# Gate and z projections as one 512-column product, a branch hint and neighbouring value products, in a four-layer kernel

## The chip, the cores and the metric

The kernel runs on one core of a Trainium2 chip. The metric is the device time of one execution in microseconds. TensorE (PE, with its weight loads as PEld), VectorE (DVE), ScalarE (ACT), GpSimd (POOL) and SyncE (SP, whose queue issues the DMAs) run side by side and wait for each other by semaphores.

## The reference

256 tokens of width 1024 pass through four layers, all in float32. The first two are hybrid layers, the last two a mixing attention with a hierarchical mixture of experts. Cut to what matters:

```python
def hybrid_layer(x, ...):                         # twice
    h = rms_norm(x, norm_g)
    (qa, ka, va, za, ba, aa, ub, zb, qc, kc, vc, zc, iq, ik, iw, gates) = split_columns(h @ w_in)
    ya = deltanet_branch(qa, ka, va, za, ba, aa, ...)      # ... * silu(za)
    yb = pooling_branch(ub, zb, ...)                       # ... * silu(zb)
    yc = sparse_attention_branch(qc, kc, vc, zc, ...)      # ... * silu(zc)
    projected = einsum('btnc,ncd->btnd', stack([ya, yb, yc]), w_branch)
    gate = sigmoid(gates.reshape(b, t, 3, 1024) + gate_b)
    return x + sum(gate * projected, axis=2) @ w_out

def second_block(x, ...):                         # two layers
    h = _mixing(x, ...)       # 4 heads each: stick-breaking, forgetting, MLA, dilated (3 branches)
    x = _layernorm(alpha * x + h, ln1_g, ln1_b)
    m = _hier_moe(x, ...)     # 16 experts, two for each token
    x = _layernorm(alpha * x + m, ln2_g, ln2_b)
```

The gates have 3 x 1024 columns and za, zb, zc 512 each.

## The kernel before

**Products.** A float32 product that must be exact is done in three: both operands are split into a rounded part (`hi`, by a cast on ACT, L383) and the rest (`lo`, a subtraction on DVE or POOL, L384), and `mm3` adds hi times hi, hi times lo and lo times hi. Weights come through SP's queue in tiles `w` of 512 KB and are split on the way.

**Projections.** `proj_t` keeps the weights stationary (128 rows of the output at a time) and lets the 256 tokens move; it makes one output tile of 128x256 in 8 steps of three products. Two such tiles share a PSUM bank `pd` of 512 columns, of which there are three, and `use` reads both when the second is done. `gates` (tanh of each of 8 tiles, L951) and the calls for za, zb and zc (`silu2`, L662 and L663) go through it; the gates are multiplied into the branch products at L962 and L965. `proj_n` keeps the tokens stationary and lets 512 weight columns move.

**Attention.** `heads` handles two heads at a time and both query blocks (128 and 256 keys): softmax of a head, transposes of its weights `p` on TensorE (L368) and copies of them into `pt` on ACT (L1093, L1095). `weigh` then multiplies by the values (mv, vv, and x for the dilated heads), with two heads in the two halves of the array's columns. Forgetting, MLA and dilated heads go through it, two pairs each in a layer.

**Experts.** 16 experts are worked in pairs from slots of 64 tokens. `stream` issues the expert weights ahead of their use, into tiles that earlier stages free, in the order of `SLOTS_W` and `SLOTS_1` and with the buffers of `TWO`. At the ninth expert (`e == 8`) `overflow` has a conditional for tokens beyond the slots:

```python
n = nc.values_load(mi[0:1, 0:1], skip_runtime_bounds_check_because="compared only")
...
with tc.If(n > SLOTS):
```

Its body is skipped in these runs, so that TensorE branches over it (L1740). The router's product is made with 120 columns, six copies of 20.

**Order.** A scheduler sets the order of the instructions on each engine ahead of time, by the dependences and its own estimates; the source's order is only one input.

Of the kernel before, what the change touches and what calls it, by code (L numbers as in the profile page):

```python
# [49 lines left out]
TWO = dict(w4=18, w4b=5, w2=4, w2a=6, w2b=6, w1=2, w1a=6, w1b=4, wo=4, hi=3, lo=3)  # L50
# [3 lines left out]
SLOTS_W = [("w4", 8)] * 18 + [("w4b", 8)] * 5 + [("w2", 4)] * 4 + [("w2b", 4)] * 6 + [("ring", 8)] * RING  # L54
# [181 lines left out]
class K:  # L236
# [92 lines left out]

    def s(self, name, *shape, bufs=2, dt=F32):  # L330
        return self.sm.tile([128] + list(shape), dt, name=name, bufs=bufs)
# [74 lines left out]
    def proj_t(self, blk, l, name, act, use, per=1):  # L406

        kk = len(act[0])
        i, ps = 0, None
        for hi, lo in self.group(blk, l, name):  # L410
            v = [a.rearrange("p (k n) -> p k n", k=kk) for a in (hi, lo)]
            for j in range(per):
                if i % 2 == 0:
                    ps = self.dbank()
                o = ps[:, (i % 2) * T:(i % 2) * T + T]
                cs = slice(j * 128, j * 128 + 128)
                for k in range(kk):
                    self.mm3(o, (v[0][:, k, cs], v[1][:, k, cs]), (act[0][k], act[1][k]), k == 0, k == kk - 1)
                if i % 2:
                    use(i - 1, ps[:, 0:T])  # L420
                    use(i, o)
                i += 1
# [85 lines left out]
    def transposed(self, src, name, scale=None, bias=None, keep=True, banks=(None,)):  # L508
# [3 lines left out]
        hi, lo = self.big(name + "h", 8, F32R), self.big(name + "l", 8, F32R)  # L512
# [21 lines left out]
        return full, (hi, lo)  # L534
# [48 lines left out]
    def layer1(self, l):  # L583
# [338 lines left out]
        pt("zb", lambda i, ps: silu2(zb[:, i], ps, w1("sz")))  # L922
# [25 lines left out]
        def gates(n):  # L948
# [6 lines left out]
            pt("g%d" % n, use)  # L955
# [19 lines left out]
        pt("zc", lambda i, ps: silu2(zc[:, i], ps, w1("sz")))  # L975
# [40 lines left out]
        pt("za", lambda i, ps: silu2(za[:, i], ps, w1("sz")))  # L1016
# [23 lines left out]
    def layer2(self, l, xT, xs):  # L1040
# [37 lines left out]
        def heads(scale, logits, nbr=1, pair=None):  # L1078


            pts = [(w4("pt2")[:, :768], w2("pt1")[:, :384]) if nbr == 3 else (w2("pt")[:, :384],) for _ in range(2)]
            at = lambda j, br: pts[j][br // 2][:, (br % 2) * 384:(br % 2) * 384 + 384]

            def rest(j, qb, parts):
                S = 128 * (qb + 1)
                p = (w4 if nbr == 3 else w1)("p")[:, :nbr * S]
                self.softmax(parts, scale, p)
                for br in range(nbr):
                    pst = bank()
                    for i in range(qb + 1):  # L1090
                        self.tr(pst[:, tok(i)], p[:, br * S + i * 128:br * S + i * 128 + 128])
                    if qb:
                        A.copy(at(j, br)[:, 128:384], pst[:, 0:256])  # L1093
                    else:
                        A.copy(at(j, br)[:, 0:128], pst[:, 0:128])  # L1095

            if pair:
                for qb in range(2):
                    for j, parts in enumerate(pair(qb)):
                        rest(j, qb, parts)  # L1100
            else:
                for j in range(2):
                    for qb in range(2):
                        rest(j, qb, logits(j, qb))
            return [[at(j, br) for br in range(nbr)] for j in range(2)]
# [258 lines left out]
        for tb in range(2):  # L1364
            for k in range(8):
                self.mm(pl[:, tb * 120:tb * 120 + 120], zT[k // 4][tb][:, k % 4],
                        gw[:, k, None, :].to_broadcast([128, 6, 20]), k + tb == 0, k == 7)
# [25 lines left out]
    def moe(self, l, zh, lg):  # L1393
# [252 lines left out]
        for e in range(0, NE, 2):  # L1646
# [23 lines left out]
            if e % 4 == 2 and e + 2 < NE:  # L1670
                next_Ds, next_Db, _ = one_hot(e + 2)
                nxt = self.chunks("xg")
                for at, k in ((3, 0), (3, 2), (6, 4), (6, 6)):
                    todo_b.setdefault(at, []).append(lambda k=k: gather((k, k + 1), next_Ds, nxt))
            into_slots(e + 1, todo_b)
# [44 lines left out]
    def overflow(self, l, cnt, G2, zs, pv, sums):  # L1720
# [19 lines left out]
        with tc.If(n > SLOTS):  # L1740
# [100 lines left out]
```

## Time and profile before

| | |
|---|---|
| median of 3 runs | 1511.82 us (1511.78 to 1512.58) |
| profiled execution | 1510.49 us |
| its span | 1508.1 us |
| hybrid layers | about 0 to 645 us |
| attention stages | about 645 to 845 and 1065 to 1270 us |
| expert layers | about 845 to 1065 and 1270 to 1495 us |
| TensorE, VectorE, ScalarE busy | 97%, 53%, 44% of the span |
| mean granted clock of TensorE | 0.993 |

The span is what the trace covers; the execution's own time has some 2.4 us more around it. Names of rows are the program's tiles: `pd<-hTh,hi` is a product into bank pd of the token part hTh and the weight part hi (hTl and lo are the rests), and L349 is the line of the helper that records each product. The printed end of a product is modelled and overlaps with the next one, so its pace is read from the starts.

### The profile page before, as it was taken

To read this page: it belongs to the slowest core of one execution; us is meant where nothing else is said; L and a number is where in the kernel's file an instruction comes from. 1 tells how busy PE (TensorE), PEld (TensorE's weight loads), DVE (VectorE), ACT (ScalarE), POOL (GpSimd) and SP (SyncE) were. 2 spreads that over 40 slices of the span, in tenths; PEclk is the share of its full clock that TensorE was granted. 3 is DMA by queue.
4 is the path that set the end of the run, shared out by engine and by line. 5 is a ranking of instruction groups with operands and counts; after the bars stand their busy time and mean duration, and the time that the engine had idled before them with its cause. 6 is when DMAs were issued, how large, how long until landed. Compare 5 with 4: busy or idle time off the path is not lost. (4 is left out here: it accounts for less than half of the span.)

```text
span 1508.1 us, 25410 instructions
## 1 busy us (share of the span) xinstructions
PE 1461.3 (97%) x9770; PEld 1074.5 (71%) x9770; DVE 802.5 (53%) x1865; ACT 667.2 (44%) x1359; POOL 87.2 (6%) x94
## 2 busy tenths in 40 slices
PE   8999999999999999999999999899899999998996
PEld 7878999989788999987777644343677877443442
DVE  5878656669768556766754511111656655211113
ACT  6635545557555455456564311111465563111111
POOL 3300000111100000020000100000100001000000
PEclk9999999999999999999999999999999999999998
DMA  7522664555225655544578889999334778989994
GB/s 270 170 59 66 206 184 140 179 156 178 88 62 166 192 160 163 175 129 152 165 269 292 296 344 396 406 408 404 118 118 145 247 264 311 361 346 404 404 405 167
DMA packets 108144, 345.49 MB, mean 229 GB/s; under 512 B 12144, under 2 KB 16880, under 8 KB 108016
## 3 DMA queue, kind: packets, MB, share of 16 engines
q1 hardware_dynamic: 108016, 343.79, 65.5%
q8 instruction: 80, 1.31, 0.3%
q14 instruction: 48, 0.39, 0.1%
HBM read 342.69 MB, written 1.05 MB: 228 GB/s over the span
## 5 line engine op out<-in xcount | busy, mean ns | idle before, releaser
L384 DVE TENSOR_TENSOR lo<-w,hi 128x1024 fp32r<-128x1024 f32 (+3 forms) x243 | 298.6, 1229 | 164.8 <-ACT hi L383 160.2
L383 ACT CAST hi<-w 128x1024 fp32r<-128x1024 f32 (+2 forms) x258 | 268.0, 1039 | 230.7 <-PE pd L349 182.6
L349 PE MATMUL p<-w,xg 128*64 128x512 f32 (+1 forms) x1028 | 234.9, 595 | 8.1 <-issue 4.1
L349 PE MATMUL pd<-hTh,hi 128*128 128x256 f32 x768 | 218.7, 285 | 0.0
L349 PE MATMUL pd<-hTl,hi 128*128 128x256 f32 x768 | 218.2, 284 | 0.0
L349 PE MATMUL pd<-hTh,lo 128*128 128x256 f32 x768 | 218.2, 284 | 0.0
L349 PEld LDWEIGHTS p<-w,xg 128*64 128x64 f32 x1028 | 72.8, 137 | 130.3 <-issue 110.4
L349 PEld LDWEIGHTS pd<-hTl,hi 128*128 128x128 f32 x768 | 147.2, 192 | 0.2
L349 PEld LDWEIGHTS pd<-hTh,hi 128*128 128x128 f32 x768 | 147.2, 192 | 0.2
L349 PEld LDWEIGHTS pd<-hTh,lo 128*128 128x128 f32 x768 | 147.2, 192 | 0.1
L349 PE MATMUL p<-w,hTe 128*64 128x512 f32 x512 | 117.8, 594 | 0.0
L1626 DVE SCALAR_TENSOR_TENSOR yl<-p,gslot,yh 128x512 fp32r<-128x512 f32 x32 | 24.0, 751 | 143.4 <-ACT yh L1625 116.3
L349 PEld LDWEIGHTS p<-w,hTe 128*64 128x64 f32 x512 | 37.0, 137 | 72.2 <-issue 64.6
L349 PE MATMUL pd<-hi,xTh 128*128 128x512 f32 (+2 forms) x224 | 87.2, 389 | 0.1
L349 PE MATMUL pd<-hi,xTl 128*128 128x512 f32 (+2 forms) x224 | 86.5, 388 | 0.0
L349 PE MATMUL pd<-lo,xTh 128*128 128x512 f32 (+2 forms) x224 | 85.4, 381 | 0.0
L1580 ACT COPY a<-p 128x512 f32<-128x512 f32 x32 | 18.8, 586 | 147.1 <-PE p L349 146.6
L1590 DVE SCALAR_TENSOR_TENSOR t<-t,p 128x256 f32<-128x256 f32 x32 | 13.4, 419 | 122.2 <-ACT t L1589 113.8
L1625 ACT ACTIVATE yh<-p,gslot 128x512 fp32r<-128x512 f32 x32 | 22.0, 688 | 101.0 <-PE p L349 87.7
L349 PE MATMUL pd<-hi,hTl 128*128 128x512 f32 (+1 forms) x160 | 63.4, 398 | 0.0
L349 PE MATMUL pd<-lo,hTh 128*128 128x512 f32 (+1 forms) x160 | 61.9, 387 | 0.5 <-POOL lo L384 0.5
L349 PE MATMUL pd<-hi,hTh 128*128 128x512 f32 (+1 forms) x160 | 62.1, 388 | 0.0
(540 smaller groups left out, 2780.9 us busy)
## 6 DMA issues: line engine op xcount, KB each, us to landing
w<-in_we SPq DMA_DIRECT2D x320, 512.0 KB, 8.9
w<-in_p SPq DMA_DIRECT2D x244, 512.0 KB, 3.7
w<-in_we SPq DMA_DIRECT2D x110, 256.0 KB, 6.4
w<-in_p SPq DMA_DIRECT2D x8, 420.0 KB, 3.5
w<-in_we SPq DMA_DIRECT2D x20, 128.0 KB, 5.3
x<-in_we SPq DMA_DIRECT2D x4, 512.0 KB, 4.0
w<-in_p SPq DMA_DIRECT2D x4, 498.0 KB, 4.9
x<-in_x SPq DMA_DIRECT2D x4, 256.0 KB, 4.1
```

Source lines behind the costliest of these rows:

```text
L349: self.last = self.nc.tensor.matmul(out, lhsT, rhs, start=start, stop=stop, skip_group_check=True)
L383: r = self.nc.scalar.copy(hi, a)
L384: (eng or self.nc.vector).tensor_tensor(lo, a, hi.bitcast(F32), op=OP.subtract)
L1580: A_.copy(a, ps)
L1590: V.scalar_tensor_tensor(t, t, 1.0, ps[:, :, 0:64], op0=OP.add, op1=OP.mult)
L1625: A_.activation(yh, ps, AF.Copy, scale=gs)
L1626: V.scalar_tensor_tensor(yl, ps, gs, yh.bitcast(F32), op0=OP.mult, op1=OP.subtract)
```

## The change

Four edits:

1. For the gates and za, zb, zc the two token parts lie side by side in one tile (`parts`), and the high weights multiply both in one product of 512 columns; the low weights times the high tokens are added onto the second half. The two halves are added behind: ACT copies the first out of the bank, DVE adds the second. Each output tile then has a bank of its own, and tanh and silu read the sum from SBUF.
2. TensorE gets a hint that the branch over the overflow's body is likely taken.
3. `heads` takes both heads of a query block together: their transposes go to one bank, one ACT copy takes them out, and all transposes of a block stand together. Buffers `w4` fall from 18 to 15 and `w4b` rise from 5 to 8.
4. The router's product has 20 columns, not 120.

```diff
@@ -47,11 +47,11 @@
 
 ONE = dict(w4=14, w4s=2, w2=4, w2n=11, w2s=1, w1=14, w1n=13, w1s=3, hi=3, lo=3, j=1)
 ONE_P = dict(pd=3, p=2, pn=3)
-TWO = dict(w4=18, w4b=5, w2=4, w2a=6, w2b=6, w1=2, w1a=6, w1b=4, wo=4, hi=3, lo=3)
+TWO = dict(w4=15, w4b=8, w2=4, w2a=6, w2b=6, w1=2, w1a=6, w1b=4, wo=4, hi=3, lo=3)
 MIX_P = dict(pd=2, p=1, pa=2, pb=3)
 MOE_P = dict(p=4, pacc=4)
 
-SLOTS_W = [("w4", 8)] * 18 + [("w4b", 8)] * 5 + [("w2", 4)] * 4 + [("w2b", 4)] * 6 + [("ring", 8)] * RING
+SLOTS_W = [("w4", 8)] * 15 + [("w4b", 8)] * 8 + [("w2", 4)] * 4 + [("w2b", 4)] * 6 + [("ring", 8)] * RING
 
 SLOTS_1 = [("wo", 8)] * 2 + [("hi", 8), ("lo", 8)] + [("w1", 2)] * 2 + [("w1a", 2)] * 6 + [("w1b", 2)] * 2 + [("w2a", 4)] * 5 + [("x", 8)] * 2
 
@@ -327,6 +327,13 @@
         ts = [self.w4(name, 4, T, dt=dt) for _ in range((n + 3) // 4)]
         return [ts[i // 4][:, i % 4] for i in range(n)]
 
+    def parts(self, name, n):
+
+
+        ts = [self.w4(name, 2, 2 * T, dt=F32R) for _ in range((n + 1) // 2)]
+        both = [ts[i // 2][:, i % 2] for i in range(n)]
+        return [a[:, :T] for a in both], [a[:, T:] for a in both], both
+
     def s(self, name, *shape, bufs=2, dt=F32):
         return self.sm.tile([128] + list(shape), dt, name=name, bufs=bufs)
 
@@ -403,9 +410,22 @@
         for j, n in enumerate(ns):
             yield self.piece(self.I["p%d" % blk][l, i0 + j, :, :n], n, name)
 
-    def proj_t(self, blk, l, name, act, use, per=1):
+    def proj_t(self, blk, l, name, act, use, per=1, into=None):
+
 
         kk = len(act[0])
+        if into:
+            for i, (hi, lo) in enumerate(self.group(blk, l, name)):
+                v = [a.rearrange("p (k n) -> p k n", k=kk) for a in (hi, lo)]
+                ps = self.dbank()
+                for k in range(kk):
+                    self.mm(ps, v[0][:, k], act[2][k], k == 0, False)
+                    self.mm(ps[:, T:], v[1][:, k], act[0][k], False, k == kk - 1)
+                o = into(i)
+                self.nc.scalar.copy(o, ps[:, :T])
+                self.nc.vector.tensor_tensor(o, o, ps[:, T:], op=OP.add)
+                use(i, o)
+            return
         i, ps = 0, None
         for hi, lo in self.group(blk, l, name):
             v = [a.rearrange("p (k n) -> p k n", k=kk) for a in (hi, lo)]
@@ -509,7 +529,7 @@
 
         V, A, G = self.nc.vector, self.nc.scalar, self.nc.gpsimd
         full = self.big(name, 8) if keep else [None] * 8
-        hi, lo = self.big(name + "h", 8, F32R), self.big(name + "l", 8, F32R)
+        parts = hi, lo, _ = self.parts(name + "p", 8)
         col = lambda a, c: a[:, c:c + 1]
         for c in range(8):
             ps = self.bank(banks[c % len(banks)])[:, :T]
@@ -531,7 +551,7 @@
         if keep and bias is None:
             for c in range(8):
                 G.tensor_tensor(full[c], hi[c].bitcast(F32), lo[c].bitcast(F32), op=OP.add)
-        return full, (hi, lo)
+        return full, parts
 
     def rope(self, dst, src, cos, sin, half):
 
@@ -919,7 +939,7 @@
         V.tensor_scalar(hps, pv["pool_scale"], 0.5, None, op0=OP.mult)
         ob = (w4("obh", 4, T, dt=F32R), w4("obl", 4, T, dt=F32R))
         zb = w4("zb", 4, T)
-        pt("zb", lambda i, ps: silu2(zb[:, i], ps, w1("sz")))
+        pt("zb", lambda i, o: silu2(o, o, w1("sz")), into=lambda i: zb[:, i])
         pls = []
         for g in (0, 2):
             ps = bank("pn").rearrange("p (g n) -> p g n", g=2)
@@ -952,7 +972,7 @@
                 if n == 0 and j == 7:
                     self.preload(LOG_EXP, r)
 
-            pt("g%d" % n, use)
+            pt("g%d" % n, use, into=lambda j: gt[n][j])
 
         def branch(n, br, last):
             act = ([br[0][:, j] for j in range(4)], [br[1][:, j] for j in range(4)])
@@ -972,7 +992,7 @@
         gates(1)
         branch(1, ob, False)
         zc = w4("zc", 4, T)
-        pt("zc", lambda i, ps: silu2(zc[:, i], ps, w1("sz")))
+        pt("zc", lambda i, o: silu2(o, o, w1("sz")), into=lambda i: zc[:, i])
         gates(2)
 
         sel = []
@@ -1013,7 +1033,7 @@
 
         self.sub = ""
         za = w4("za", 4, T)
-        pt("za", lambda i, ps: silu2(za[:, i], ps, w1("sz")))
+        pt("za", lambda i, o: silu2(o, o, w1("sz")), into=lambda i: za[:, i])
         oa = (w4("oah", 4, T, dt=F32R), w4("oal", 4, T, dt=F32R))
         for ch in range(2):
             ps = bank4()
@@ -1078,31 +1098,20 @@
         def heads(scale, logits, nbr=1, pair=None):
 
 
-            pts = [(w4("pt2")[:, :768], w2("pt1")[:, :384]) if nbr == 3 else (w2("pt")[:, :384],) for _ in range(2)]
-            at = lambda j, br: pts[j][br // 2][:, (br % 2) * 384:(br % 2) * 384 + 384]
-
-            def rest(j, qb, parts):
+            pts = [w4("pt")[:, :768].rearrange("p (j n) -> p j n", j=2) for _ in range(nbr)]
+            for qb in range(2):
                 S = 128 * (qb + 1)
-                p = (w4 if nbr == 3 else w1)("p")[:, :nbr * S]
-                self.softmax(parts, scale, p)
+                ps_ = []
+                for j, parts in enumerate(pair(qb) if pair else [logits(j, qb) for j in range(2)]):
+                    ps_.append((w4 if nbr == 3 else w1)("p")[:, :nbr * S])
+                    self.softmax(parts, scale, ps_[j])
                 for br in range(nbr):
-                    pst = bank()
-                    for i in range(qb + 1):
-                        self.tr(pst[:, tok(i)], p[:, br * S + i * 128:br * S + i * 128 + 128])
-                    if qb:
-                        A.copy(at(j, br)[:, 128:384], pst[:, 0:256])
-                    else:
-                        A.copy(at(j, br)[:, 0:128], pst[:, 0:128])
-
-            if pair:
-                for qb in range(2):
-                    for j, parts in enumerate(pair(qb)):
-                        rest(j, qb, parts)
-            else:
-                for j in range(2):
-                    for qb in range(2):
-                        rest(j, qb, logits(j, qb))
-            return [[at(j, br) for br in range(nbr)] for j in range(2)]
+                    pst = bank().rearrange("p (j n) -> p j n", j=2)
+                    for j in range(2):
+                        for i in range(qb + 1):
+                            self.tr(pst[:, j, tok(i)], ps_[j][:, br * S + i * 128:br * S + i * 128 + 128])
+                    A.copy(pts[br][:, :, 128:384] if qb else pts[br][:, :, 0:128], pst[:, :, :S])
+            return [[pts[br][:, j] for br in range(nbr)] for j in range(2)]
 
         def weigh(g, pts, values):
             parts = []
@@ -1363,8 +1372,7 @@
         pl = bank("p")
         for tb in range(2):
             for k in range(8):
-                self.mm(pl[:, tb * 120:tb * 120 + 120], zT[k // 4][tb][:, k % 4],
-                        gw[:, k, None, :].to_broadcast([128, 6, 20]), k + tb == 0, k == 7)
+                self.mm(pl[:, tb * 120:tb * 120 + 20], zT[k // 4][tb][:, k % 4], gw[:, k], k + tb == 0, k == 7)
         self.warm(WR, "pb")
         lg, sh = s("elg", 2, 20, bufs=1), s("esh", 2, 20, bufs=1)
         for tb in range(2):
@@ -1672,6 +1680,8 @@
                 nxt = self.chunks("xg")
                 for at, k in ((3, 0), (3, 2), (6, 4), (6, 6)):
                     todo_b.setdefault(at, []).append(lambda k=k: gather((k, k + 1), next_Ds, nxt))
+            if e == 6:
+                tc.mark_branch_hint_location(f"spare{l}", hint="LikelyTaken", engines=[mybir.EngineType.PE])
             into_slots(e + 1, todo_b)
             if e % 4 == 2 and e + 2 < NE:
                 Ds, Db, xg = next_Ds, next_Db, nxt
@@ -1737,7 +1747,7 @@
         ps = self.bank().rearrange("p (a n) -> p a n", a=2)
         x1 = [self._t(tag, 1024, "x1", (4, T), F32) for tag in ("hi", "lo")]
         x1 = [x1[k // 4][:, k % 4] for k in range(8)]
-        with tc.If(n > SLOTS):
+        with tc.If(n > SLOTS, label=f"spare{l}"):
             for k in range(8):
                 for tb in range(2):
                     for i, z in enumerate(zs[tb]):
```

The order on ScalarE in the first gates of a hybrid layer before (`hi<-w` is the cast of a weight tile, `gt<-pd` a gate's tanh):

```order
L383 CAST obh<-obt 128x256 x3
L383 CAST hi<-w 128x1024 x2
L951 ACTIVATE gt<-pd,hgb 128x256 x2
L383 CAST hi<-w 128x1024 x2
L951 ACTIVATE gt<-pd,hgb 128x256 x2
```

And in the changed kernel, where `gt<-pd` is the copy of the first half:

```order
L390 CAST obh<-obt 128x256 x3
L390 CAST hi<-w 128x1024
L425 COPY gt<-pd 128x256
L971 ACTIVATE gt<-gt,hgb 128x256
L425 COPY gt<-pd 128x256
L390 CAST hi<-w 128x1024
L971 ACTIVATE gt<-gt,hgb 128x256
L390 CAST hi<-w 128x1024
```

Two tanh in a row, with two casts between the pairs, have become a copy, a tanh and a cast for each tile.

The order on TensorE around the first value products of an MLA head pair before (`pb<-pt,mv`; `pd` are projection products):

```order
L368 MATMUL pb<-fc,p 128x128 x2
L349 MATMUL pb<-pt,mv 64x256
L349 MATMUL pd<-hi,xTh 128x512
L349 MATMUL pb<-pt,mv 64x256
L349 MATMUL pb<-pt,mv 64x128 x2
```

And in the changed kernel:

```order
L356 MATMUL pd<-lo,xTp 128x512
L356 MATMUL pd<-hi,xTp 128x512 x2
L356 MATMUL pb<-pt,mv 64x256 x2
L356 MATMUL pb<-pt,mv 64x128 x2
L356 MATMUL pd<-hi,xTp 128x512
```

The four products of the pair stand together, and no transpose is right ahead of them.

The order on TensorE behind the conditional of the first expert layer before (the rows up to the branches at L1746 belong to the body):

```order
L349 MATMUL pacc<-oy,fc 128x512 x2
L1746 REGISTER_ALU
L1746 COMPARE_AND_BRANCH
L1746 UNCONDITIONAL_BRANCH
L1740 UNCONDITIONAL_BRANCH
L349 MATMUL p<-w,xg 64x512 x4
```

And in the changed kernel:

```order
L356 MATMUL pacc<-oy,fc 128x512 x2
L1756 REGISTER_ALU
L1756 COMPARE_AND_BRANCH
L1756 UNCONDITIONAL_BRANCH
L1750 UNCONDITIONAL_BRANCH
L1847 BRANCH_PREFETCH_HINT
L356 MATMUL p<-w,xg 64x512 x4
```

The hint for the second layer's branch stands right behind the first branch, a whole layer ahead of its own. The one for the first layer stands at the program's start on TensorE:

```order
L1847 UNCONDITIONAL_BRANCH
L1847 BRANCH_PREFETCH_HINT
L356 LDWEIGHTS warmer
L356 MATMUL pd<-warmer 128x512
L356 LDWEIGHTS warmer
```

Neither stands at the seventh expert, where the source has it.

## Rows read from the trace of the kernel before

**Rows 1.** Page, part 1: busy us of each engine, share of the span, instructions.

```profile
PE 1461.3 (97%) x9770; PEld 1074.5 (71%) x9770; DVE 802.5 (53%) x1865; ACT 667.2 (44%) x1359; POOL 87.2 (6%) x94
```

**Rows 2.** Waits of TensorE, whole span: total us, times, longest us.

```profile
PE p L349 <- issue: 4.1, 1, 4.1
PE p L349 <- PEq L1740: 3.9, 1, 3.9
PE p L349 <- ACT pl L930: 3.5, 2, 1.8
...
PE pa L368 <- DVE x L1692: 2.4, 1, 2.4
```

**Rows 3.** Timeline of TensorE in the gates: start us, us, instruction, tiles.

```profile
179.74 0.28 PE L349 MATMUL pd<-hTh,hi 128*128 128x256 f32 x1
...
181.42 0.28 PE L349 MATMUL pd<-hTh,lo 128*128 128x256 f32 x1
```

**Rows 4.** Timeline of TensorE in the output projection, 512-column products of the same type.

```profile
825.64 0.39 PE L349 MATMUL pb<-lo,og 128*128 128x512 f32 x1
...
827.91 0.39 PE L349 MATMUL pd<-hi,og 128*128 128x512 f32 x1
```

**Rows 5.** Gate tile gt, its readers: ns min/median/max, first and last start us.

```profile
L951 ACT ACTIVATE gt<-pd,hgb x48: 465/469/472, 175.8 to 599.7; 128x256 f32<-128x256 f32 x48
...
L962 DVE SCALAR_TENSOR_TENSOR mg<-gt,pd x16: 412/418/422, 195.1 to 520.7; 128x256 f32<-128x256 f32 x16
```

**Rows 6.** Windows beside gates and z: busy us (count) by engine, clock, DMA.

```profile
150.00:170.00 20.00, 17.56 (x134) 16.79 (x133) 17.35 (x51) 12.12 (x19) 0.00 (x0) 1.00 0.58 188
...
575.00:595.00 20.00, 20.00 (x170) 20.00 (x168) 11.88 (x14) 10.75 (x17) 0.00 (x0) 1.00 0.57 174
```

**Rows 7.** Timeline around the first branch, all engines.

```profile
946.54 0.59 ACT L1580 COPY a<-p 128x512 f32<-128x512 f32 x1 [0.51 <-PEq L1740]
947.38 0.13 PEld L349 LDWEIGHTS p<-w,xg 128*64 128x64 f32 x1 [1.82 <-ACT a L1580]
950.58 1.97 PE L349 MATMUL p<-w,xg 128*64 128x512 f32 x4 [4.13 <-issue]
```

**Rows 8.** Timeline around the second branch, all engines.

```profile
1375.88 0.59 ACT L1580 COPY a<-p 128x512 f32<-128x512 f32 x1 [0.51 <-PE p L349]
...
1379.71 1.49 PE L349 MATMUL p<-w,xg 128*64 128x512 f32 x4 [3.93 <-PEq L1740]
```

**Rows 9.** Windows: after the first branch, second attention stage, end of the first.

```profile
950.00:975.00 25.00, 24.43 (x112) 9.49 (x113) 3.66 (x9) 2.73 (x5) 0.75 (x2) 0.93 1.03 409
1070.00:1270.00 200.00, 195.65 (x1150) 154.54 (x1149) 122.60 (x299) 118.50 (x258) 7.93 (x9) 1.00 0.62 206
...
785.00:845.00 60.00, 58.29 (x375) 46.65 (x374) 32.48 (x91) 29.75 (x61) 6.46 (x9) 1.00 0.79 277
```

**Rows 10.** Timeline of TensorE: the router's 120-column products.

```profile
834.69 3.51 PE L349 MATMUL p<-gw,zT 128*128 128x120 f32 x30
```

**Rows 11.** Timeline of TensorE: one-column products of the deltanet branch.

```profile
87.35 1.84 PE L349 MATMUL pn<-fc,z 128*128 128x1 f32 x16
```

**Rows 12.** Timeline around a head pair's value products (pt, mv).

```profile
719.40 0.65 PE L349 MATMUL pb<-pt,mv 128*64 128x256 f32 x2
...
719.98 0.50 PE L349 MATMUL pd<-hi,xTh 128*128 128x512 f32 x1
...
720.41 0.86 PE L349 MATMUL pb<-pt,mv 128*64 128x256 f32 x6
...
721.21 0.50 PE L349 MATMUL pd<-lo,xTh 128*128 128x512 f32 x1
```

**Rows 13.** Timeline of TensorE: dilated value products (pt, x), with transposes between.

```profile
796.84 0.86 PE L349 MATMUL pb<-pt,x 128*64 128x256 f32 x6
...
798.74 1.30 PE L349 MATMUL pb<-pt,x 128*64 128x256 f32 x10
799.97 0.70 PE L349 MATMUL pa<-fqk 64*128 64x256 f32 x4
```

**Rows 14.** The same DMAs on SP's queue: start us, us, count.

```profile
1455.13 19.68 SPq L1425 DMA_DIRECT2D w<-in_we  x18
```

**Rows 15.** DMA issues from 1455 us on: count, KB, median us to landing.

```profile
w<-in_we SPq DMA_DIRECT2D x18, 512.0 KB, 10.2
```

**Rows 16.** TensorE: the last expert products (first row of their end).

```profile
1493.07 1.93 PE L349 MATMUL p<-w,hTe 128*64 128x512 f32 x6
```

**Rows 17.** Lines: last step of softmax, 256 columns: busy us, mean ns, idle.

```profile
L570 DVE TENSOR_SCALAR p<-p,mx 128x256 f32<-128x256 f32 x24 | 8.4, 352 | 0.5
```

## Prediction

> **What bounds the kernel now.** I read the page's engine shares first, then the waits of TensorE, then windows over the stages. In the first the reader is to see TensorE busy for 1461.3 of 1508.1 us [rows 1]: what shortens its own stream shortens the kernel, nearly one for one, and work put on ScalarE or VectorE is free until one of them makes TensorE wait. In the second he is to see how little waiting there is to win: the largest single stops are the two at the conditional of each expert layer, 4.1 and 3.9 us [rows 2]. No row there names a weight DMA. So I price the change by what it takes out of TensorE's stream and out of those two stops, and then ask what it makes late.
>
> **Gates and z.** In the gates, 256-column products start from 179.74 to 181.42 us, 14 steps in 1.68 us, one per 120 ns [rows 3]. Products of 512 columns of the same number type start from 825.64 to 827.91, 10 steps in 2.27 us, one per 227 ns [rows 4]. A triple of 256 columns costs 3 x 120 = 360 ns, the new pair 227 + 120 = 347: 13 ns less. There are 36 changed output tiles in a layer (24 gate, 12 z), 8 steps in each, two layers: 576 x 13.3 ns = **7.7 us**.
>
> The Trainium skill speaks against this: "TensorE: Matmul & The Clock Gate", section Back-to-back issue gap, gives a product's gap as N/2.4 + 2.5 ns. By it three products of 256 need 328 ns and the pair 325, and an estimate for all 576 would be 1.5 us. The rows do not follow it: they show 120 and 227, so more for each product, whatever its columns, than the rule gives.
>
> The halves must now be added: per tile an ACT copy and a DVE addition of 128x256. The nearest rows are the gate's tanh from the same banks, 469 ns, and a DVE operation with one operand from them, 418 ns [rows 5]. In a stretch full of gates (575 to 595 us, 20 us) ScalarE is busy for 10.75 us and VectorE for 11.88 [rows 6]; seven tiles in it add 3.3 and 2.9. Both stay under 15 of 20, so I take the cost as 0. The one stretch with little room is 150 to 170 us, where VectorE has 17.35 of 20 [rows 6] and the four z tiles of the pooling branch add 1.7, which fills it to 19. The waits for pl (3.5 us in both layers, [rows 2]) stand there and may grow; without the cover each of the eight such tiles would cost its DVE operation, 3.4 us in all. I allow 0 to 3.4 and take 1. A bank now holds one tile, not two, with three banks. A tile lasts 8 x 347 ns = 2.8 us, so a bank may be read for 5.6 us after its tile ends; copy and addition need 0.9 of work behind at most one cast and one subtraction each.
>
> **The branch.** At the first conditional TensorE stands idle for 4.13 us before 950.58 [rows 7], at the second 3.93 before 1379.71 [rows 8]. Not all of it is the branch. The next product needs the bank that ACT's copy empties; at the first that copy runs from 946.54 for 0.59 us, and the weight load of the next product is in place at 947.38, after which nothing that the profile shows holds the product back until 950.58 [rows 7]. So a branch of no cost gives about 950.58 - 947.5 = 3.1 us. At the second the copy ends at 1376.47 [rows 8]; with the same 0.3 us behind it, 1379.71 - 1376.75 = 3.0.
>
> After each stop the granted clock falls. The 25 us from 950 have a mean of 0.93 [rows 9]; between full (2.4 GHz) and half (1.2) that is 25 x 0.07 x 2 = 3.5 us at half speed, in which 1.7 us of work is lost. A stop of 2.4 us, that for x of line 1692 [rows 2], lies at the start of the second attention stage, in a window that keeps 1.00 [rows 9]. With a remaining stop of about 1 us the clock should stay up. Sum if the hint works: 3.1 + 3.0 + 2 x 1.7 = **9.5 us**; if not, 0. The hint costs nothing visible: one instruction, twice.
>
> Does it work? The rows say that the wait is for instructions ("issue", and the sequencer at the line of the conditional, [rows 2]), which is what a prefetch would take away. But the order shows the first hint at the program's start and the second directly behind the first conditional, each thousands of instructions before its branch. I take 0.65 for a mark that is kept until its branch comes. The Trainium skill, "Runtime: NRT & Kernel Launch", section Instruction fetch mechanics, calls the instruction memory a FIFO filled in order, in which a taken branch out of the window forces a fetch: by that rule a target fetched so early has long been pushed out, and the gain is 0. The trace agrees with the stop at the branch; nothing in it shows a hint at work.
>
> **Value products.** The four products of a head pair come in pairs that run side by side in the two halves of the array if they are neighbours. Before, at 719.40, the first stands alone, a projection product is between, and the stretch to 721.21 lasts 1.81 us [rows 12]. Less 0.23 for that product it is 1.58 us for 8 records. Unbroken, ten records of this kind take 799.97 - 798.74 = 1.23, so 0.12 each and 1.0 for eight [rows 13]: 0.6 saved in each of six groups in the order, 3.6 us. A dilated group is broken by transposes: 20 records from 796.84 to 799.97, 0.156 each; at 0.123, its 24 save 0.8, in four groups 3.2. Together 6.8 at best. Some of it is only moved (the transposes still need their own time), so I take **5**, between 2 and 6.8. The ACT copies fall from 64 to 32 wider ones, off the path.
>
> **Router.** 30 products of 120 columns take 3.51 us, 112 ns each with the last one's tail off [rows 10]; 16 products of one column take 1.84, 107 each [rows 11]. Columns do not set the pace there: 64 x 5 ns = 0.3 us at most. I take 0.
>
> **The expert weights.** They are read ahead into freed tiles, at 409 GB/s with the DMA engines full [rows 9], and arrive ever closer to their use. In the second layer the last issue ends at 1474.81 [rows 14], lands 10.2 us later [rows 15], at 1485.0, and is used at 1493.07 [rows 16]: 8 us of lead. A hint's 4.7 us leaves 3. The three slots moved from w4 to w4b come free later in attention; with what is queued behind them on SP's queue I estimate eight blocks of 512 KB, 4 MB, 10 us of DMA time at 409 GB/s. In 785 to 845 us the DMA engines are 0.79 busy [rows 9], so 12.6 us are free for it. I allow 0 to 2 us and take 1.
>
> **Sum.** 7.7 + 9.5 + 5 - 1 - 1 = 20.2 us. The profiled execution took 1510.49; the median of the runs is 1511.82, 1.3 more. Against the median that is 1491.6.
>
> **Rivals.**
> - *The hint does nothing.* The rest is 10.7 us: 1501 us. For it: the distance of the hints in the order, and nothing in the trace that shows one at work. Against: the stop is plainly one for instructions.
> - *Both heads' softmax before the first transpose.* The new loop takes both heads of a query block before it transposes. There are 12 head pairs and 24 such places. If TensorE has nothing else there, each waits for one more softmax: its last step alone is 352 ns [rows 17], with maximum, exponential and reciprocal about 1.3 us (an estimate of four such steps). All 24 open cost 31 us, and the kernel ends at 1523, slower. It is slower by more than the measurement can tell (0.2%, 3 us) from about 18 open places on, no faster from 14. Against it: VectorE and ScalarE have idle time throughout the second attention stage (122.6 and 118.5 us busy of 200), and TensorE waits little there, 4.4 of 200 [rows 9]; projection products stand between.
> - *The weights come late.* If the free 12.6 us do not take up the moved DMAs, the lead goes and the expert layers give back up to the 9.5 us: 1501 again, with a DMA in TensorE's waits.
>
> **How the numbers follow.** The sum as worked out: 0.58, with 1487 to 1495 as its own range (value products 2 to 6.8, the z wait 0 to 3.4, weights 0 to 2). Hint without effect: 0.26, 1498 to 1504. Late weights: 0.03. Attention order, partly (1506 to 1514): 0.06; fully, slower: 0.07. The likeliest gives 1491.6. From 1486 to 1504 the first three lie inside but for some 0.05 at their ends: 0.82. Faster 0.87, the same 0.06, slower 0.07.
>
> **What would show it.** Right: products of 512 and 256 columns 227 and 120 ns apart in the gates, a gate tile in 2.8 us; idle at both conditionals near 1 us and the clock 1.00 behind; value products of a pair starting within 10 ns of each other; the router unchanged. Wrong: idle of 4 us again at the conditionals; waits of TensorE for gt's or z's addition, for p at the softmax's last step, or for w.

## The result: 1496.5 us, and the profile after

The changed kernel takes 1496.5 us (median of 4 runs, 1494.94 to 1497.03), the one before 1511.91: ratio 0.9895, 95% interval 0.9878 to 0.9913, or 13 to 18 us less. It is faster, by 15 us where 20 were forecast. The profiled execution is the slowest of the four, 1497.03; that of the kernel before, 1510.49, lies below all of its other runs, so the two traces are only 13.5 us apart.

Page of the changed kernel, span and part 1 (busy us, share, instructions):

```profile
span 1495.4 us, 24405 instructions
PE 1455.4 (97%) x9193; PEld 1046.5 (70%) x9194; DVE 828.0 (55%) x1937; ACT 682.9 (46%) x1391; POOL 88.4 (6%) x94
```

Waits of TensorE in it (total us, times, longest):

```profile
PE p L356 <- ACT pl L950: 4.8, 2, 2.5
...
PE pa L375 <- DVE x L1702: 2.4, 1, 2.4
...
PE p L356 <- DVEq L1750: 1.3, 1, 1.3
...
PE pb L375 <- ACT p L584: 1.0, 2, 0.5
...
PE p L356 <- ACTq L1750: 0.7, 1, 0.7
```

Against [rows 2] the reader is to see the two stops at the conditional, 4.1 and 3.9 us, gone down to 1.3 and 0.7, and the wait for pl up from 3.5 to 4.8. No weight DMA and no softmax step has become a wait of note.

Timelines of TensorE in the changed kernel, in the z tiles of the first layer:

```profile
157.62 0.40 PE L356 MATMUL pd<-hTp,hi 128*128 128x512 f32 x1
157.86 0.28 PE L356 MATMUL pd<-hTp,lo 128*128 128x256 f32 x1
157.98 0.40 PE L356 MATMUL pd<-hTp,hi 128*128 128x512 f32 x1
...
161.51 0.40 PE L356 MATMUL pd<-hTp,hi 128*128 128x512 f32 x1
```

11 pairs take 161.51 - 157.62 = 3.89 us, 354 ns each. Forecast from [rows 3, 4] were 347. The wide product is 240 ns ahead of the narrow one, not 227. But later, in other gate tiles of the same execution and with the same products in turn:

```profile
263.05 0.39 PE L356 MATMUL pd<-hTp,hi 128*128 128x512 f32 x1
263.28 0.28 PE L356 MATMUL pd<-hTp,lo 128*128 128x256 f32 x1
...
266.87 0.39 PE L356 MATMUL pd<-hTp,hi 128*128 128x512 f32 x1
```

Here 11 pairs take 266.87 - 263.05 = 3.82 us, the 347 ns that were forecast. Of the 60 changed tiles at full clock whose products no other product breaks, 14 take 347 or 348 ns for a pair (260 to 280 and 486 to 506 us) and 46 take 351 to 354; the mean is 352. Before, the unbroken tiles take 361 ns for a triple in the mean (median 360).

Behind the two branches (first and second expert layer):

```profile
941.88 1.08 PE L356 MATMUL p<-w,xg 128*64 128x512 f32 x4
943.06 0.59 ACT L1588 COPY a<-p 128x512 f32<-128x512 f32 x1 [0.51 <-PEq L1750]
944.24 1.94 PE L356 MATMUL p<-w,xg 128*64 128x512 f32 x8 [1.28 <-DVEq L1750]
```

```profile
1368.14 0.59 ACT L1588 COPY a<-p 128x512 f32<-128x512 f32 x1 [0.51 <-PEq L1750]
1368.72 0.23 PEld L356 LDWEIGHTS p<-w,xg 128*64 128x64 f32 x4 [1.56 <-ACTq L1750]
1368.75 1.94 PE L356 MATMUL p<-w,xg 128*64 128x512 f32 x8 [0.71 <-ACTq L1750]
```

The next product comes 0.6 us and, in the second layer, directly behind the end of ACT's copy; in [rows 7, 8] it came 3.4 and 3.2 us behind it.

Windows of the changed kernel (busy us by engine, granted clock, DMA):

```profile
165.00:170.00 5.00, 3.09 (x10) 2.39 (x10) 3.84 (x10) 4.12 (x8) 0.00 (x0) 0.78 0.84 312
480.00:485.00 5.00, 2.65 (x6) 2.19 (x7) 3.29 (x9) 3.33 (x7) 0.00 (x0) 0.69 0.83 283
830.00:835.00 5.00, 4.98 (x38) 3.95 (x37) 2.56 (x14) 3.84 (x7) 1.28 (x2) 0.84 1.02 409
835.00:840.00 5.00, 4.26 (x29) 3.62 (x30) 3.85 (x13) 2.09 (x2) 5.00 (x8) 0.82 0.96 322
940.00:945.00 5.00, 3.72 (x24) 2.34 (x25) 1.09 (x2) 1.71 (x3) 0.00 (x0) 1.00 1.04 415
1065.00:1070.00 5.00, 4.29 (x24) 4.09 (x25) 4.38 (x9) 4.37 (x9) 1.49 (x2) 0.66 0.40 125
1368.00:1378.00 10.00, 9.29 (x52) 3.93 (x52) 2.36 (x8) 1.94 (x4) 0.74 (x2) 1.00 1.02 406
```

The clock (1.00 is 2.4 GHz, half of it 1.2) is now full behind both branches, where it had 0.93 over 25 us in [rows 9]. But it falls at four places where it did not before: behind the wait for pl in both hybrid layers, behind the router, and at the start of the second attention stage. It is at half for (1 - 0.84 + 1 - 0.82) x 5 x 2 = 3.4 us at the router, and as long at 1065.

Where the 12.7 us between the spans (1508.1 and 1495.4) arose is read from the starts of the same products in both traces:

| up to | before | after | gained in the stage |
|---|---|---|---|
| end of the hybrid layers (first pd<-bc) | 644.09 | 640.98 | 3.11 |
| first expert product (p<-w,xg) | 845.28 | 841.80 | 0.37 |
| end of the first expert layer (last pd<-bc) | 1070.74 | 1062.93 | 4.33 |
| first expert product of the second expert layer (p<-w,xg) | 1274.62 | 1266.88 | -0.07 |
| last pacc<-yl,gT | 1496.90 | 1484.29 | 4.87 |

The expert layers gave 9.2 us, nearly what the branches were to give (9.5); the hybrid layers gave 3.1 of the 6.7 forecast (0.4 of it before the first product pd<-hT, at 21 us), and the two attention stages with their routers 0.3 of 5. From its first projection product (pd<-hi,xT) to the last of the output projection each attention stage gains 1.1 us. It is lost again around that stretch: 0.6 us at the start of the second stage, and 0.7 and 0.5 us between the router's products and the first expert product.

### The profile page after: what moved, and what is told of

Read it like the earlier page. It is cut to its first block, busy times and chain, and to the rows that moved or that the text cites. A ratio compares the mean times of both kernels' runs of the same rounds, so it can differ in the third digit from the quotient of the medians.

```text
span 1495.4 us, 24405 instructions
## 1 busy us (share of the span) xinstructions
PE 1455.4 (97%) x9193; PEld 1046.5 (70%) x9194; DVE 828.0 (55%) x1937; ACT 682.9 (46%) x1391; POOL 88.4 (6%) x94
## 5 line engine op out<-in xcount | busy, mean ns | idle before, releaser
L356 PE MATMUL pd<-hTp,hi 128*128 128x512 f32 (+1 forms) x960 | 276.6, 354 | 0.0
L356 PE MATMUL pd<-hTp,lo 128*128 128x256 f32 x768 | 218.8, 285 | 0.0
L356 PEld LDWEIGHTS pd<-hTp,hi 128*128 128x128 f32 x960 | 168.8, 190 | 24.7
L356 PEld LDWEIGHTS pd<-hTp,lo 128*128 128x128 f32 x768 | 146.0, 190 | 0.5
L356 PE MATMUL pd<-hi,xTp 128*128 128x512 f32 (+2 forms) x448 | 142.1, 388 | 0.0
L356 PE MATMUL pd<-hi,hTp 128*128 128x512 f32 (+1 forms) x320 | 101.8, 392 | 0.0
L356 PEld LDWEIGHTS pd<-hi,xTp 128*128 128x128 f32 x448 | 81.3, 188 | 16.6 <-issue 3.7
L356 PE MATMUL pd<-lo,xTp 128*128 128x512 f32 (+2 forms) x224 | 85.2, 381 | 0.0
L356 PEld LDWEIGHTS pd<-hi,hTp 128*128 128x128 f32 x320 | 57.9, 190 | 9.6
L356 PE MATMUL pd<-lo,hTp 128*128 128x512 f32 (+1 forms) x160 | 61.8, 386 | 0.5 <-POOL lo L391 0.5
L509 DVE TENSOR_SCALAR xg<-p,pv 128x256 f32<-128x256 f32 x32 | 17.3, 542 | 57.8 <-ACT xg L515 57.8
```

Source lines behind the costliest of these rows:

```text
L356: self.last = self.nc.tensor.matmul(out, lhsT, rhs, start=start, stop=stop, skip_group_check=True)
L509: nc.vector.tensor_scalar(dst, ps, scale, bias, op0=OP.mult, op1=OP.add)
```

## The experiments

All ratios are against runs of the kernel before on the same chip; g1_single and g2_single_r120 ran on another chip than the e and f kernels, so that they are compared with those by their ratios. The first four kernels are the kernel before with one part of the change each.

**e1_hint, the branch hint alone.**

```diff
+            if e == 6:
+                tc.mark_branch_hint_location(f"spare{l}", hint="LikelyTaken", engines=[mybir.EngineType.PE])
...
-        with tc.If(n > SLOTS):
+        with tc.If(n > SLOTS, label=f"spare{l}"):
```

> The kernel before with the branch hint alone, all else as it was. My theory: the two stops at the conditional shrink from 4.1 and 3.9 us to about 1 and the clock stays at full behind them, so 8.5 to 10 us less (about 1502.5 us). Rival: the hint counts only with the shorter program of the changed kernel, whose branches and targets lie otherwise; then the stops stay and the time is that of before.

1500.79 us, ratio 0.9931 (0.9914 to 0.9948): 8 to 13 us less. Its windows over the place of both branches:

```profile
947.00:957.00 10.00, 9.68 (x52) 4.08 (x54) 2.15 (x7) 1.39 (x4) 0.74 (x2) 1.00 1.03 409
...
1372.00:1382.00 10.00, 9.68 (x52) 4.07 (x54) 2.15 (x7) 1.64 (x4) 0.74 (x2) 1.00 1.03 406
```

TensorE waits 1.0 and 0.7 us there and the clock stays full. The hints stand at the program's start and behind the first branch here too, so the distance does not keep them from working, and the rival of the shorter program falls. By the starts of the products, 4.6 us are gained in the first expert layer and 4.9 in the second, 9.5 together.

**e2_router20, the narrow router alone.**

```diff
-                self.mm(pl[:, tb * 120:tb * 120 + 120], zT[k // 4][tb][:, k % 4],
-                        gw[:, k, None, :].to_broadcast([128, 6, 20]), k + tb == 0, k == 7)
+                self.mm(pl[:, tb * 120:tb * 120 + 20], zT[k // 4][tb][:, k % 4], gw[:, k], k + tb == 0, k == 7)
```

> The kernel before with the router's product of 20 columns alone. My theory, from the trace of the changed kernel, where the granted clock fell at 830 to 840 us, right behind the router: the narrow products let the clock fall to half in one or both expert layers, at 3.4 us of half speed and 1.7 us of loss each, so 1.5 to 3.5 us more than before. Rival: the fall there has another cause (the order of what stands around the router); then no difference, at most 0.3 us less.

1512.04 us, ratio 1.0003 (0.9994 to 1.0013): no difference that can be told. The profile shows the fall in the first layer (0.67 from 835 to 840 us), none behind the second router. So my theory had a place right and the price wrong: the interval reaches from 0.9 us less to 2.0 more, which leaves little of the 1.5 to 3.5 expected. Over its ten executions the mean granted clock is 0.990, over the 22 of the kernel before on that chip 0.992, which is some 6 us more at half speed in each execution (31 against 25) and still no time that can be told.

**e3_heads, the order of the heads and the buffers alone** (the diff of `heads`, `TWO` and `SLOTS_W`).

> The kernel before with the new order in heads and the new buffers alone. Prediction on record: 5 us less (2 to 6.8). From the trace of the changed kernel, where the attention stages gave only 1.0 and 1.4 us: 2 to 3 us less, and no new fall of the clock. Rival: the neighbouring products save their 5 us, and something else in the changed kernel ate them there.

1507.64 us, ratio 0.9974 (0.9962 to 0.9985): 2 to 6 us less. That looks like the forecast, but the starts say otherwise: each attention stage gains 1.1 us, 2.2 together. The first expert layer gains 2.0, at its conditional and without any hint. Timeline of TensorE there:

```profile
943.90 1.08 PE L349 MATMUL p<-w,xg 128*64 128x512 f32 x4
945.95 1.47 PE L349 MATMUL p<-w,xg 128*64 128x512 f32 x5 [0.97 <-DVEq L1729]
949.47 1.07 PE L349 MATMUL p<-w,xg 128*64 128x512 f32 x3 [2.05 <-issue]
```

Behind the branch five products run after 0.97 us, the wait that the hint leaves too, and only then comes a stop of 2.05 us with nothing named; in [rows 7] the stop of 4.13 came before the first one. Together 3.02 us, 1.1 less, and the clock stays at 1.00 behind it. At the second branch the stop is 4.0 us as before.

The new order and the new buffers could be the reason as well as the place of the code. The trace of e2_router20, which changes neither, settles it:

```profile
944.97 1.08 PE L349 MATMUL p<-w,xg 128*64 128x512 f32 x4
947.01 0.61 PE L349 MATMUL p<-w,xg 128*64 128x512 f32 x1 [0.97 <-DVEq L1739]
950.51 3.68 PE L349 MATMUL p<-w,xg 128*64 128x512 f32 x7 [2.88 <-issue]
```

Counted over the trace's records of TensorE, the first branch is number 14077 before, 14074 in e2_router20 and 14066 in e3_heads: 3 and 11 earlier. The stop comes 1 and 5 products later, which with their weight loads are 2 and 10 records. So it sits at the same place of the code, but for one record, and an edit that shifts the branch against that place shortens the stop. In all three traces a 16 KB packet of the instruction queue (q8 of the DMA view) lands some 1.4 us before the product that ends the stop: at 949.23 before, 949.06 and 948.02. In e1_hint one lands too, at 949.39, and TensorE does not wait; that the hint only brings the fetch forward is not shown.

**e4_gates, the wide products alone** (`parts`, `proj_t` and its six calls).

> The kernel before with the 512-column products for gates and z alone. Prediction on record: 7.7 us less by the pace, 1 lost at the pooling branch. From the trace of the changed kernel: a pair takes 354 ns instead of the 347 forecast, which gives 3.3 us less; the wait for pl in the pooling branch is longer and the clock falls behind it in both layers, 1.7 us each, so the sum is 3 us less to no change. Rival: the clock falls there only with the other parts; then 3.3 us less or more and no half-speed stretch at 165 and 482 us.

1508.36 us, ratio 0.998 (0.9971 to 0.999): 1.5 to 4.4 us less. Pairs take 347 to 354 ns here too, 351 in the mean of the unbroken tiles, and the clock falls at 165 and at 480 us, with pl waited for 4.8 us:

```profile
165.00:170.00 5.00, 2.56 (x10) 1.81 (x9) 4.25 (x11) 3.63 (x7) 0.00 (x0) 0.85 0.72 257
480.00:485.00 5.00, 2.65 (x8) 2.02 (x7) 3.52 (x9) 3.16 (x6) 0.00 (x0) 0.75 0.77 278
```

The rival, that the falls need the other parts, is out. The time meets the top of my range, but not by my sum: the pace gave more than the 3.3 us that I had taken from one place, and the falls cost less than 1.7 us each (below).

**f1_grouped, f2_zb_old, f3_both.** The changed kernel with the wide products of a tile ahead of its narrow ones; with zb on the way of before; with both.

```diff
                 for k in range(kk):
                     self.mm(ps, v[0][:, k], act[2][k], k == 0, False)
+                for k in range(kk):
                     self.mm(ps[:, T:], v[1][:, k], act[0][k], False, k == kk - 1)
...
-        pt("zb", lambda i, o: silu2(o, o, w1("sz")), into=lambda i: zb[:, i])
+        pt("zb", lambda i, ps: silu2(zb[:, i], ps, w1("sz")))
```

> The changed kernel with the eight 512-column products of an output tile first and its eight 256-column products behind them, instead of in turn. My theory: the turn of wide and narrow products is what makes a pair take 354 ns; grouped, the wide ones come every 227 ns and the narrow ones every 120, so 347 together and 4 us less than the changed kernel (about 1492). Rival: the wide products are slower because of their operand (235 ns grouped too); then the pair stays at 354 and the time at 1496.

1496.25 us, ratio 0.9897 (0.988 to 0.9913), as the changed kernel. Timeline of TensorE in its gates:

```profile
206.91 2.00 PE L356 MATMUL pd<-hTp,hi 128*128 128x512 f32 x8
208.75 1.12 PE L356 MATMUL pd<-hTp,lo 128*128 128x256 f32 x8
209.71 2.00 PE L356 MATMUL pd<-hTp,hi 128*128 128x512 f32 x8
```

A tile takes 209.71 - 206.91 = 2.80 us in this place, 350 ns for a pair: wide 230, narrow 120. In 58 of 60 unbroken tiles it is 349. Against the 352 of the tiles in turn that is 3 ns, some 1.5 us over 576 pairs, so the turn explains part of what is missing to 347, and the tiles that ran at 347 in turn it does not explain. The time did not show it, with pl waited for 5.4 us, a fall of the clock more in this profile (1260 us) and one less (482).

> The changed kernel with zb, the z tiles of the pooling branch, on the way of before (three products of 256 columns, two tiles to a bank, silu read from the bank). My theory: the copy and the addition of these four tiles stand ahead of the copy of pl on ScalarE and VectorE; without them the wait for pl is 1.8 us again, the clock stays up at 165 and 482 us, and the kernel gains 1.7 us of clock and 0.6 of wait in each layer less 0.2 of pace, so 3 to 4 us. Rival: the fall comes from the one stretch without products, however it is filled; then it stays and the time changes by less than 1 us.

1495.74 us, ratio 0.9894 (0.9877 to 0.991). The wait for pl is 3.5 us again. But the clock:

```profile
165.00:170.00 5.00, 3.05 (x18) 2.35 (x16) 2.74 (x5) 3.00 (x7) 0.00 (x0) 1.00 0.70 231
480.00:485.00 5.00, 3.26 (x9) 2.72 (x10) 2.61 (x5) 3.13 (x6) 0.00 (x0) 0.70 0.87 294
```

It still falls in the second layer. The 3 to 4 us expected did not come. The hybrid layers, from their first product pd<-hT (21 us) to the first projection product of the attention, gain 2.0 us on the changed kernel in the profile, but this execution is at half clock for 3.4 us more before 20 us, and its first product comes 1.9 us later.

> Both edits at once, zb on the old way and grouped products elsewhere. By both theories 6 to 8 us less than the changed kernel (about 1489 to 1490); by both rivals no difference.

1493.74 us (1493.55 to 1494.96), ratio 0.9885 (0.9868 to 0.9901): all four runs lie below all four of f1_grouped (from 1495.22), 2.5 us better in the median, not the 6 to 8 expected. No fall at 165 and 480 us in its profile, and the wait for pl is 3.5 us; between the same two products it gains 5.7 us on the kernel before, the changed kernel 2.7.

**f4_no_gates, the changed kernel without the wide products.**

> The changed kernel with its gates and z products as before: hint, heads and router only. If the parts add, the hint (10.8 us) and heads (4.0 us) give 1497, as fast as the whole change, and the wide products have brought nothing in it. If the wide products keep the 3.2 us that they had alone, this is 3 us slower than the changed kernel, 1499.5.

1500.23 us, ratio 0.9926 (0.991 to 0.9943). So the wide products keep at least what they had alone in the whole change (4.7 us by the two ratios, with wide intervals), and what does not add is heads: with the hint there it is worth, together with the router, 0.6 us on e1_hint, not 4.0. The 2.0 us at the first branch are taken away by the hint. The 1.1 us in each attention stage are there in this trace too, and 0.4 and 0.5 go again between router and first expert product.

**g1_single and g2_single_r120.** f3_both, with the forgetting heads' transposes head by head; then also the router of before. `single` is set for the forgetting heads alone.

```diff
                     self.softmax(parts, scale, ps_[j])
+                    if single:
+                        pst = bank()
+                        for i in range(qb + 1):
+                            self.tr(pst[:, tok(i)], ps_[j][:, i * 128:i * 128 + 128])
+                        A.copy(pts[0][:, j, 128:384] if qb else pts[0][:, j, 0:128], pst[:, :S])
+                if single:
+                    continue
```

What they rest on is the place of the forgetting heads' logit products (pa<-fqk). Before, the wide ones of two heads stood together, as in the last of [rows 13]. In the changed kernel:

```profile
775.83 0.70 PE L356 MATMUL pa<-fqk 64*128 64x256 f32 x2
776.45 0.49 PE L356 MATMUL pa<-fc,lf 128*128 128x128 f32 x2
...
777.66 0.70 PE L356 MATMUL pa<-fqk 64*128 64x256 f32 x2
778.29 0.49 PE L356 MATMUL pa<-fc,lf 128*128 128x128 f32 x2
```

Each head runs alone and takes 0.62 us. Before, the four records of a pair, two heads side by side, took no longer than that together, 0.63 us to the next product's start at 800.60. From start to next start the 32 records took 5.2 us before and 8.1 in the changed kernel.

> f3_both (zb on the old way, grouped products) with the forgetting heads' transposes again head by head, each in a bank of its own. In the changed kernel the logit products of the forgetting heads (pa, fqk) are no longer neighbours: 32 records took 5.2 us before and 8.1 after, which ate most of what the value products saved. In this order four of the eight pairs, the wide ones, stand together again. My theory: the 32 records fall to about 6.6 us and the kernel gains 1 to 2 us on f3_both (about 1492). Rival: the loss of the attention stages lies elsewhere (projection products spread out); then no difference.

1491.58 us, ratio 0.9869 (0.9852 to 0.9885). Timeline of TensorE in it:

```profile
774.69 0.72 PE L356 MATMUL pa<-fqk 64*128 64x256 f32 x4
775.34 0.49 PE L356 MATMUL pa<-fc,lf 128*128 128x128 f32 x2
```

The wide pairs run together again (0.65 us for both heads), the 32 records take 5.8 us, and each attention stage, from first projection product to output projection, gains 2.6 us against 1.1 in f3_both. That is 3.0 us in the trace, and 2.4 by the two ratios; the rival falls.

> The same with the router's product of 120 columns as before. In five of six profiles with 20 columns the granted clock falls behind the router of the first expert layer, in one of four with 120. If the columns keep the clock up there: 1 to 3 us less than g1_single. If the falls come by chance of the execution: no difference, and a fall is seen with 120 columns too.

1490.73 us (1490.38 to 1491.25), ratio 0.9867 (0.985 to 0.9883): the fastest kernel here, but not apart from g1_single (1490.12 to 1492.07). Its profile has no fall behind the router:

```profile
825.00:840.00 15.00, 13.33 (x100) 10.16 (x100) 10.89 (x50) 8.10 (x14) 6.46 (x9) 1.00 0.92 323
```

**The falls over all profiles.** Behind the wait for pl the clock fell at 5 of 6 places in the three profiles with zb on the new way (both layers of the changed kernel and of e4_gates, one of f1_grouped), and at 2 of 18 in the nine with the old. Behind the first router it fell in 6 of 7 profiles with 20 columns and in 1 of 5 with 120; behind the second in one of each. So both go with more falls there, and neither decides it in one execution. For the router this is not settled: alone it lowered the mean clock (e2_router20), while g1_single and g2_single_r120 have the same, 0.994 over four executions each. At the start of the second attention stage it fell in 9 of 12, under either form of every part, and did not in the profile of before that the prediction read. A fall there costs less than the 1.7 us that I took: from the end of the expert layer to the first projection product the nine profiles with one lose 0.5 to 1.0 us against before, the other two less than 0.1. In f4_no_gates, whose hybrid layers are those of before, the fall at 165 us costs 0.8.

## Why the prediction was right in sign and 5 us too low

- **Gates and z: sign right, size wrong.** The term said 13.3 ns less for each of 576 steps, 7.7 us. In unbroken tiles the runs show 361 to 352 ns, 9 ns less, and all products pd<-hT together (gates, z and 24 unchanged tiles) went from 280.4 to 275.5 us from start to next start, with the seven at half clock put at full: 4.9 us. The step that failed is the price of the wide product, which was taken from another stage. Ahead of a narrow one it takes 230 to 241 ns, and grouped with its like 230, not 227. The turn explains some 3 of the 5 ns between 352 and 347. But two stretches ran at 347 in the same turn, so neither the product nor its neighbour's width alone sets the pace; what does was not tried. The Trainium skill's rule ("TensorE: Matmul & The Clock Gate", Back-to-back issue gap), which the page gives for an isolated product and which would have made 1.5 us in all, misses the 4.9 on the other side, and the gaps that it states (109 and 216 ns) are not the pace of these rows.
- **The wait for pl: the place right, the price too low.** 1 us was allowed, 3.4 at most. The wait grew by 1.3 us, and the fall of the clock behind it, which I had not priced, came on top. From the first product pd<-hT to the first projection product of the attention the trace gains 2.7 us, 2.2 less than the pace, and I put those down to this place. My check of engine loads (VectorE 17.35 of 20 us in [rows 6]) showed the danger; the shares did not say how far the stop would grow, nor that the clock would fall behind it.
- **The branch: right.** Forecast 3.1 + 3.0 of idle and 3.4 of clock; in the changed kernel the stops lost 2.8 and 3.2 and the clock is full; by the starts of the products 9.5 us in e1_hint and 9.2 in the changed kernel. The rival that the hint does nothing falls, and so does the rule of the Trainium skill ("Runtime: NRT & Kernel Launch", Instruction fetch mechanics) as I applied it: a hint thousands of instructions ahead worked. The other half of it, that a taken branch waits for a fetch of instructions, agrees with the stop in the traces without a hint, which ends 1.4 us behind the landing of a packet of the instruction queue.
- **Value products: right by themselves.** Their own records went from 21.3 to 17.1 us from start to next start, 4.2 less where 5 were forecast; a pair's four products now take 0.80 us and not 1.58, and the two that run side by side start 6 to 7 ns apart, as TensorE's timeline in the changed kernel shows:

```profile
710.72 0.87 PE L356 MATMUL pb<-pt,mv 128*64 128x256 f32 x8
711.52 0.50 PE L356 MATMUL pd<-hi,xTp 128*128 128x512 f32 x1
```

  The step that failed is "only moved", for which I took 1.8 us off: I did not look at which other neighbours the new order parts. The forgetting heads' logits gave back 2.9 us, and g1_single got most of it again. The softmax rival, which would have made the kernel slower, did not come: TensorE waits for p 0.5 us in each layer.
- **Router: no measurable difference**, as forecast. Its products take 0.36 us less in each layer, more than the 0.3 at most for both, and between them and the first expert product g1_single loses at least as much against g2_single_r120. For a reason that I had not seen, the clock, it may have a small price.
- **Expert weights: the allowance of 1 us was not needed.** No DMA is among TensorE's waits in any profile, and the expert layers gain the same with the old buffers (e1_hint, 4.6 and 4.9 us) as with the new ones (f4_no_gates).

In the sum, from the one trace to the other: 4.9 us of pace, 2.2 lost at pl, 9.2 at the branches, 0.3 in the attention stages with their routers, and 0.4 ahead of the first product pd<-hT, 12.6 together; forecast were 7.7, 1 lost, 9.5, 5, and 1 lost to the weights. What is missing lies in the attention stages (4.7) and in the pace (2.8). The falls of the clock took their part, 0.5 to 1.0 us each where it can be read. Hint, heads and wide products measured alone (10.4, 3.9 and 3.0 us by their ratios) add to 17.3, more than the whole, because heads took part of its 3.9 from a stop that the hint removes.

The range held, but partly by luck. 1496.5 us lies outside the 1487 to 1495 that I gave the sum itself. It lies inside 1486 to 1504 because that range was made wide for a hint without effect, and the hint had its full effect.

## What to carry to other kernels

A product's pace has to be read where it will stand, with its neighbours, and in more than one stretch: wide and narrow in turn were the sum of the two alone in some tiles and up to 7 ns more in others. When products are brought together, look in the order for the pairs that are driven apart by it. And an edit measured alone can borrow its gain from another's place; here code that was only shifted gained 2 us at a branch, and the whole change tells it apart.

## What the runs showed of the hardware

- A hint to TensorE at the program's start, or a whole layer ahead of its branch, takes the instruction stop away (from 4.13 and 3.93 us of idle to 1.0 and 0.7 in e1_hint).
- Without it, what a branch costs depends on where its code lies. The same work had one stop of 4.13 us before, 0.97 and 2.88 us around one product in e2_router20, and 0.97 and 2.05 us around five in e3_heads, the second stop each time at the same place of the code.
- Products of 512 and 256 columns in turn ran at 347 ns a pair in some tiles and at up to 354 in others of the same execution.
- Stops of about 2 us bring half a clock in some profiles and not in others: 2.4 us at the start of the second attention stage went without one in the trace of before and with one (0.66 over 5 us) in the changed kernel's, where the wait was as long. The price is less than the half clock suggests: 0.5 to 1.0 us in the nine profiles with a fall there.
